# Out-projection of a trunk layer: low halves, S1 sums and one residual addition moved from GpSimd to VectorE

## The chip, the cores and the metric

One core of a Trainium2 chip runs the whole program. The metric is the device time of one execution in microseconds, lower is better. "VectorE" is DVE in the rows, "ScalarE" ACT, "GpSimd" POOL, "TensorE" PE; SP is the queue that issues the loads and stores.

## The reference

One layer, 1024 tokens of width 1024. A gated DeltaNet mixer (8 heads) and a cross-attention over 256 memory tokens (4 heads) give `y_mix` and `y_mem`; the part that matters here is what follows:

```
y = jnp.concatenate([y_mix, y_mem], axis=-1) @ w_out[layer]
h = h + rms_norm(y, norm_post_mix[layer])
f = swiglu(rms_norm(h, norm_pre_ffn[layer]), w_ffn_in[layer], w_ffn_out[layer])
h = h + rms_norm(f, norm_post_ffn[layer])
```

`y` is 1024 x 1536 times 1536 x 1024, all in float32.

## The kernel before

**Matmuls in three passes.** A float32 operand is split in two: ScalarE casts it to the short matmul type (the high half, `whi`), and another engine subtracts that from the float32 source (the low half, `wlo`). Each product is then three matmuls: high by high, high by low, low by high (`split_step`, lines 906 to 908). A matmul that reads a low half waits until its subtraction is done.

**The out-projection as seven block products.** `y` and `w_out` are cut into 2 x 2 blocks, and seven products of sums of blocks replace eight (`OPRODS`, `o_prod(j)` for j = 0 to 6). A block of the left operand (A11, A12, A21, A22) is 768 x 512, six k-blocks of 128 x 512; so is a block of the right one (B11, B12, B21, B22, and the weight sums T1 to T4, made early in the program and kept in DRAM). Product j takes six steps k. A step loads the A block and the B block (`o_operands`), has ScalarE cast both (line 890), makes both low halves (line 891), and then issues 4 x 3 matmuls into four accumulators. The high and low tiles have three buffers each, so the split can be at most about two steps ahead of TensorE.

In `o_operands` the two low halves go to different engines, the A block's to GpSimd and the B block's to VectorE:

```
for i, (src, eng) in enumerate(zip(srcs, (nc.gpsimd, nc.vector))):
    nc.scalar.copy(hi[:, i], src)
    last_lo[i] = eng.tensor_tensor(out=lo[:, i], in0=src, in1=hi[:, i].bitcast(F32), op=ALU.subtract).ins
```

**Sums of blocks.** `o_sums(1, k)` makes A11 - A21 on VectorE and S1 = A21 + A22 on GpSimd beside product 1; product 2 needs A22 - (A11 - A21) (`o_operands`, j = 2), product 3 uses S1 and makes a further difference of A12. All are additions of 128 x 512 tiles through the helper `add` (line 854). The blocks A21 and A22 lie in tiles named oB11h, oB11l and oB21h, two k-blocks of each in each tile.

**Results and residuals.** `o_combine` adds a finished accumulator (PSUM) to the partial results `hn` on VectorE, beside the first four steps of the next product, and ScalarE sums squares. In products 5 and 6 `post_stage` finishes the first half of the tokens, and behind product 6 the second half, one tile of 128 tokens at a time: three small GpSimd operations make `rstd` (lines 961, 83, 85), VectorE scales (line 965, 128 x 1024), then the residual `xr` is added (line 966, through `add`, 128 x 1024) and stored; ScalarE squares it (line 973), GpSimd makes the next `rstd`, ScalarE scales (line 981), and the tile's buffer can take the next load of `x`. `ON_POOL` lists the tiles, as (half, n), whose residual addition runs on GpSimd: one, (1, 0).

**What else runs there.** Beside product 0 the cross-attention still runs; beside products 1 to 3 the weights of the first FFN tile are prepared (`gate_w`, `up_w`: scaling at line 1057 and differences at line 1095 on VectorE, low halves at lines 93 and 1078 on GpSimd). Behind product 6 come the first FFN products `m1` and `m2`, whose second weight tile has its low half on VectorE (line 93), and the transposes of the normed tokens.

**Order.** Each engine takes its instructions in one order, fixed when the program is built: a scheduler places them from the order in the code and its own estimates, so moving an operation to another engine also moves its neighbours. An engine waits at the head of its queue.

In the rows the products start on TensorE at 688.84 us (0), 716.16 (1), 740.06 (2), 763.64 (3), 779.96 (4), 796.28 (5), 822.15 (6), and product 6 ends at 842.43.

Of the kernel before, what the change touches and what calls it, by code (L numbers as in the profile page):

```python
# [10 lines left out]
F32 = mybir.dt.float32  # L11
# [3 lines left out]
ALU = mybir.AluOpType  # L15
# [24 lines left out]

ON_POOL = ((1, 0),)
OB = 8
FILL = 2
TFILL = (3, 4)
# [8 lines left out]
def trunk_kernel(ctx: ExitStack, tc: tile.TileContext, a: dict, out: bass.AP):  # L55
    nc = tc.nc
# [122 lines left out]
    for tn in range(NT):  # L179
# [23 lines left out]
        for q in range(2):  # L203
            pt = bank(("ms", "iv")[q], "pt")
            for j in range(4):
# [3 lines left out]
            hi = uhi[hf][:, q * 4:q * 4 + 4, n * P:(n + 1) * P]  # L209
            nc.scalar.copy(hi, p3)  # L210
            nc.vector.tensor_tensor(out=ulo[hf][:, q * 4:q * 4 + 4, n * P:(n + 1) * P], in0=p3,
                                    in1=hi.bitcast(F32), op=ALU.subtract)
# [172 lines left out]
    def tmp(name):  # L385
# [38 lines left out]
                            in1=gc.rearrange("p h n -> p (h n)"), op=ALU.subtract)  # L424
# [428 lines left out]
    def add(out, x, y, eng=nc.vector, op=ALU.add):  # L853
        return eng.tensor_tensor(out=out, in0=x, in1=y, op=op)  # L854

    def load_block(t, name, k):
        if name[0] == "A":
            i, j = int(name[1]) - 1, int(name[2]) - 1
            src = y_d[k + KH * j][:, HO[i] * HF:(HO[i] + 1) * HF]
        else:  # L860
            src = t_d[name][k] if name[0] == "T" else wo_block(int(name[1]), int(name[2]), k)
        nc.sync.dma_start(t, src)

    def o_raw():
        return wp.tile([P, 2, HF], F32, tag="raw", name="raw", bufs=2)

    def block(name, k):
        if (name, k) not in oblk:
            t = yp.tile([P, HF], F32, name=f"{name}_{k}", bufs=1) if name in YP else free_slots.pop(0)
            oblk[name, k] = t  # L870
            load_block(t, name, k)
        return oblk[name, k]

    def o_operands(j, k):
        an, bn = OPRODS[j]
        first = j == 0 and k < 2
        raw = o_raw() if j == 6 or first else None
        if j == 2:

            add(block("A22", k), block("A22", k), block("A11", k), op=ALU.subtract)  # L880
        if raw is None:
            srcs = [block(an, k)]
        else:
            srcs = [raw[:, 0]]
            load_block(raw[:, 0], an, k)
        srcs.append(raw[:, 1] if first else yp.tile([P, HF], F32, tag="ob", name="ob", bufs=OB))
        load_block(srcs[1], bn, k)
        hi, lo = (wp.tile([P, 2, HF], F32R, tag="w" + c, name="w" + c, bufs=3) for c in ("hi", "lo"))
        for i, (src, eng) in enumerate(zip(srcs, (nc.gpsimd, nc.vector))):
            nc.scalar.copy(hi[:, i], src)  # L890
            last_lo[i] = eng.tensor_tensor(out=lo[:, i], in0=src, in1=hi[:, i].bitcast(F32), op=ALU.subtract).ins  # L891
        return hi, lo

    last_lo = [None, None]

    def o_sums(j, k):

        if j == 1:
            add(block("A11", k), block("A11", k), block("A21", k), op=ALU.subtract)
            add(block("A21", k), block("A21", k), block("A22", k), nc.gpsimd)  # L900
        elif j == 3:
            add(block("A12", k), block("A12", k), block("A22", k), op=ALU.subtract)

# [46 lines left out]
    def post_stage(i, half, n):  # L950
# [12 lines left out]
        elif i == 1:  # L963
            xr, rs = post[n]
            nc.vector.scalar_tensor_tensor(out=hn, in0=hn, scalar=rs, in1=grow[0], op0=ALU.mult, op1=ALU.mult)
            ins = add(xr, hn, xr, nc.gpsimd if (half, n) in ON_POOL else nc.vector).ins
            if (half, n) not in ON_POOL:
                last_h[0] = ins
# [38 lines left out]
    def o_prod(j):  # L1007
        acc = [bank((("pj", "sc"), ("ms", "iv"))[j % 2][n // 2], f"acc{j}") for n in range(4)]
        held = []
        for k in range(KH):  # L1010
            hl = o_operands(j, k)
            with tc.issue_after(last_lo[0]), tc.issue_after(last_lo[1]):
                o_sums(j, k)
                if j and k < 4:
                    o_combine(j - 1, k, oprev[0][k])
                if j >= 5:
                    t = k + KH * (j - 5)
                    for i in range(4):
                        post_stage(i, 0, t - POST[i])
            if j == 6 and k >= KH - TAIL:  # L1020
                held.append((k, hl))
                continue
            for n in range(4):
                mm = split_step(acc, n, k == 0, k == KH - 1, *hl)
                if j == 6 and k >= FILL:
                    with tc.issue_after(mm.ins):
                        next(fill, None)
# [440 lines left out]
```

## Time and profile before

| What | Value |
|---|---|
| Timed runs (3) | 1551.32, 1548.78, 1543.25 us; median 1548.78 |
| Profiled execution | 1535.88 us, span of its instructions 1533.7 us |
| Mean granted TensorE clock | 0.984 of full speed |
| Busy over the span | VectorE 1068.4 us (70%), ScalarE 682.1 (44%), GpSimd 825.6 (54%) |
| DMA | 168.13 MB, mean 110 GB/s |

The busy times are for the whole program; the out-projection, from 688.84 to 842.43 us, is a tenth of it. The profiled execution is one run of its own and lies 12.9 us below the median of the timed ones. A row's duration runs from an instruction's start to its end as recorded; where instructions follow each other without a gap, the distance of their starts is the better price.

### The profile page before, as it was taken

Reading aid. Unit: us, or ns where it says so; the run is one execution under the profiler, and the core shown is the slowest. Engines: PE = TensorE matmul, PEld = TensorE weight load, DVE = VectorE, ACT = ScalarE, POOL = GpSimd, SP = SyncE. Lnnn points to the kernel's source line nnn. Section 1 sums busy time; section 2 is a strip of 40 time slices with the busy share of each in tenths; the row PEclk is TensorE's granted clock in tenths of the full one; section 3 lists DMA queues with packets and bytes.
Section 4 is the critical chain, followed back from the end, with each engine's and each line's share of the span. In section 5 each row is a group of like instructions: output and inputs, shape, how many; then the busy total and the mean of one; then the engine's idle time right before and its main releaser. Section 6 shows DMA issues by size and latency. Waiting matters only on the chain.

```text
span 1533.7 us, 22655 instructions
## 1 busy us (share of the span) xinstructions
PE 1468.6 (96%) x8237; PEld 1207.5 (79%) x8237; DVE 1068.4 (70%) x1651; ACT 682.1 (44%) x1481; POOL 825.6 (54%) x705
## 2 busy tenths in 40 slices
PE   7999999999999999999798789999999999999996
PEld 5778888888888888887686668888888887778784
DVE  7555767677676867667977877666666665685967
ACT  7565555555555554345346532222222222444352
POOL 3543646474646544204756556666666665554455
PEclk9999999999999999999899899999999999999998
DMA  6411222222212220219334222222222223973334
GB/s 203 158 56 38 67 70 93 72 85 63 90 63 77 78 73 29 83 64 308 109 103 158 82 90 104 103 103 103 104 103 103 104 103 125 317 251 96 90 103 159
DMA packets 77553, 168.13 MB, mean 110 GB/s; under 512 B 10433, under 2 KB 12929, under 8 KB 77442
## 3 DMA queue, kind: packets, MB, share of 16 engines
q1 hardware_dynamic: 76720, 165.58, 32.1%
q8 instruction: 64, 1.05, 0.3%
q10 hardware_dynamic: 722, 1.12, 0.2%
q14 instruction: 47, 0.39, 0.1%
HBM read 124.42 MB, written 42.24 MB: 109 GB/s over the span
## 4 chain that ended last, share of the span: by engine, by line
PE 35%; DVE 5%; POOL 4%; issue 3%; DMA 2%; ACT 2%; DVEq 0%; SPq 0%; POOLq 0%; ACTq 0%
PE fo L907 3%; PE fo L908 3%; PE fo L906 3%; PE sc L137 3%; PE sc L135 2%; PE sc L136 2%; PE iv L135 2%; PE iv L137 2%; PE iv L136 2%; PE pj L136 2%; PE pj L137 2%; PE pj L135 2%; POOL wlo L891 2%; DVE B L854 1%; PE ms L136 1%
## 5 line engine op out<-in xcount | busy, mean ns | idle before, releaser
L246 PE MATMUL pj<-uhi,whi 128*128 128x512 f32 x496 | 216.3, 436 | 0.0
L93 POOL TENSOR_TENSOR wlo<-raw,whi 128x1024 fp32r<-128x1024 f32 x61 | 157.5, 2581 | 77.4 <-ACT whi L92 76.9
L246 PE MATMUL pj<-uhi,wlo 128*128 128x512 f32 x496 | 196.0, 395 | 0.0
L246 PE MATMUL pj<-ulo,whi 128*128 128x512 f32 x496 | 195.0, 393 | 0.0
L295 DVE SCALAR_TENSOR_TENSOR cv<-cb,convw_sb,cv 128x512 f32<-128x512 f32 x144 | 148.3, 1030 | 23.1 <-ACT cv L290 22.4
L1292 POOL TENSOR_TENSOR wlo<-ar,whi 128x512 fp32r<-128x512 f32 x75 | 106.4, 1421 | 98.0 <-ACT whi L1291 97.8
L907 PE MATMUL fo<-wlo,whi 128*128 128x512 f32 x308 | 123.3, 400 | 8.3 <-DVE wlo L1292 8.1
L908 PE MATMUL fo<-whi,wlo 128*128 128x512 f32 x308 | 120.8, 393 | 0.0
L906 PE MATMUL fo<-whi 128*128 128x512 f32 x308 | 118.4, 391 | 0.6 <-DVE c L854 0.6
L92 ACT CAST whi<-raw 128x1024 fp32r<-128x1024 f32 x66 | 69.6, 1054 | 106.1 <-DVE raw L1057 50.8
L1292 DVE TENSOR_TENSOR wlo<-B,whi 128x512 fp32r<-128x512 f32 x75 | 83.1, 1110 | 45.7 <-ACT whi L1291 45.1
L246 PEld LDWEIGHTS pj<-uhi,wlo 128*128 128x128 f32 x496 | 93.5, 189 | 21.5
L246 PEld LDWEIGHTS pj<-ulo,whi 128*128 128x128 f32 x496 | 94.4, 190 | 11.2
L246 PEld LDWEIGHTS pj<-uhi,whi 128*128 128x128 f32 x496 | 94.1, 190 | 11.3 <-issue 0.2
L1095 DVE TENSOR_TENSOR raw<-raw 128x512 f32<-128x512 f32 x86 | 84.8, 986 | 25.6 <-POOL wlo L93 17.1
L1057 DVE TENSOR_TENSOR raw<-raw,gcols_sb 128x1024 f32<-128x1024 f32 x44 | 67.2, 1527 | 50.0 <-DMA raw<-in_w_ffn_in 50.0
L1291 ACT CAST whi<-ar 128x512 fp32r<-128x512 f32 x75 | 46.5, 621 | 112.4 <-POOL wlo L1292 75.4
L907 PE MATMUL acc<-wlo,whi 128*128 128x512 f32 x168 | 69.1, 411 | 12.6 <-DVE wlo L891 12.6
L907 PEld LDWEIGHTS fo<-wlo,whi 128*128 128x128 f32 x308 | 58.1, 189 | 28.8 <-DVE wlo L1292 17.2
L1078 POOL TENSOR_TENSOR plo<-raw,phi 128x1024 fp32r<-128x1024 f32 (+1 forms) x22 | 52.7, 2397 | 46.2 <-ACT phi L1077 44.8
L908 PE MATMUL acc<-whi,wlo 128*128 128x512 f32 x168 | 68.7, 409 | 2.4 <-POOL wlo L891 2.4
L906 PEld LDWEIGHTS fo<-whi 128*128 128x128 f32 x308 | 58.2, 189 | 13.5 <-DVE c L854 1.0
(408 smaller groups left out, 4214.3 us busy)
## 6 DMA issues: line engine op xcount, KB each, us to landing
raw<-in_w_ffn_in SPq DMA_DIRECT2D x44, 512.0 KB, 3.3
raw<-in_w_in SPq DMA_DIRECT2D x36, 512.0 KB, 3.3
ar<-g_S SPq DMA_DIRECT2D x44, 256.0 KB, 2.6
B<-in_w_ffn_out SPq DMA_DIRECT2D x42, 256.0 KB, 4.7
g_A<-g SPq DMA_DIRECT2D x33, 256.0 KB, 2.0
ar<-g_A SPq DMA_DIRECT2D x29, 256.0 KB, 4.0
wsum<-in_w_out SPq DMA_DIRECT2D x24, 256.0 KB, 4.2
T_d<-wsum SPq DMA_DIRECT2D x24, 256.0 KB, 2.0
```

Source lines behind the costliest of these rows:

```text
L92: nc.scalar.copy(hi, raw)
L93: (lo_eng or nc.gpsimd).tensor_tensor(out=lo, in0=raw, in1=hi.bitcast(F32), op=ALU.subtract)
L135: nc.tensor.matmul(ps, whi, uhi, start=first, stop=False)
L136: nc.tensor.matmul(ps, whi, ulo, start=False, stop=False)
L137: return nc.tensor.matmul(ps, wlo, uhi, start=False, stop=last)
L246: ins = nc.tensor.matmul(*args, **kw)
L295: nc.vector.scalar_tensor_tensor(out=cf, in0=cb[:, c0:c0 + HF], scalar=w[:, j:j + 1], in1=cf, op0=ALU.mult, op1=ALU.add)
L906: nc.tensor.matmul(acc[n], hi[:, 0, ts_], hi[:, 1], start=first, stop=False)
L907: nc.tensor.matmul(acc[n], hi[:, 0, ts_], lo[:, 1], start=False, stop=False)
L908: return nc.tensor.matmul(acc[n], lo[:, 0, ts_], hi[:, 1], start=False, stop=last)
L1095: nc.vector.tensor_tensor(out=o, in0=x, in1=y, op=op)
L1292: last_lo[i] = eng.tensor_tensor(out=lo[:, i], in0=src, in1=hi[:, i].bitcast(F32), op=ALU.subtract).ins
```

## The change

All low halves of the out-projection, both operands' in all seven products, are made on VectorE (42 instructions that were GpSimd's), S1 as well (6), and no residual addition is left on GpSimd (1).

```
-ON_POOL = ((1, 0),)
+ON_POOL = ()
...
-        for i, (src, eng) in enumerate(zip(srcs, (nc.gpsimd, nc.vector))):
+        for i, src in enumerate(srcs):
             nc.scalar.copy(hi[:, i], src)
-            last_lo[i] = eng.tensor_tensor(out=lo[:, i], in0=src, in1=hi[:, i].bitcast(F32), op=ALU.subtract).ins
+            last_lo[i] = nc.vector.tensor_tensor(out=lo[:, i], in0=src, in1=hi[:, i].bitcast(F32), op=ALU.subtract).ins
...
         if j == 1:
             add(block("A11", k), block("A11", k), block("A21", k), op=ALU.subtract)
-            add(block("A21", k), block("A21", k), block("A22", k), nc.gpsimd)
+            add(block("A21", k), block("A21", k), block("A22", k))
```

VectorE in product 1, a piece of the difference (A_0 to A_2 are k-blocks of A11, A_3_8880 and A_4_8907 are of product 1's A12, `ob` is a B block, `oB11h` and `oB11l` hold A21 and A22):

```order
 L854 TENSOR_TENSOR A_0_8805<-A_0_8805,oB11h 128x512
-L891 TENSOR_TENSOR wlo<-ob,whi 128x512
+L854 TENSOR_TENSOR oB11h<-oB11h 128x512
+L891 TENSOR_TENSOR wlo<-A_3_8880,whi 128x512
 L854 TENSOR_TENSOR A_1_8834<-A_1_8834,oB11h 128x512
+L891 TENSOR_TENSOR wlo<-ob,whi 128x512
+L854 TENSOR_TENSOR oB11h<-oB11h 128x512
+L854 TENSOR_TENSOR A_2_8671<-A_2_8671,oB11l 128x512
+L891 TENSOR_TENSOR wlo<-A_4_8907,whi 128x512
+L854 TENSOR_TENSOR oB11l<-oB11l 128x512
```

Between two low halves of the B blocks there are now an S1 sum, a difference and the low half of an A block.

VectorE in product 5, before (acc_9257 is product 4's last accumulator, `hn` the partial results, `xr` a residual tile, `rstd` the row scale):

```order
L854 TENSOR_TENSOR hn<-acc_9257,hn 128x512
L965 SCALAR_TENSOR_TENSOR hn<-hn,rstd,grow_8786 128x1024
L891 TENSOR_TENSOR wlo<-ob,whi 128x512
L965 SCALAR_TENSOR_TENSOR hn<-hn,rstd,grow_8786 128x1024
L854 TENSOR_TENSOR xr<-hn,xr 128x1024
L891 TENSOR_TENSOR wlo<-ob,whi 128x512 x2
L854 TENSOR_TENSOR xr<-hn,xr 128x1024
```

and the same place now:

```order
L854 TENSOR_TENSOR hn<-acc_9257,hn 128x512
L965 SCALAR_TENSOR_TENSOR hn<-hn,rstd,grow_8786 128x1024
L891 TENSOR_TENSOR wlo<-A_4_8715,whi 128x512
L854 TENSOR_TENSOR xr<-hn,xr 128x1024
L891 TENSOR_TENSOR wlo<-ob,whi 128x512
L965 SCALAR_TENSOR_TENSOR hn<-hn,rstd,grow_8786 128x1024
L891 TENSOR_TENSOR wlo<-A_5_8737,whi 128x512
L891 TENSOR_TENSOR wlo<-ob,whi 128x512
L891 TENSOR_TENSOR wlo<-raw,whi 128x512
L854 TENSOR_TENSOR xr<-hn,xr 128x1024
```

The low halves of the A blocks stand between the residual operations, and the addition of the third tile has moved ahead of a low half and of the fourth tile's scaling.

VectorE behind product 6 (acc_9605 and acc_9606 are its last two accumulators, `c_9927` the first `m2` result, `wlo<-raw` the low half of the second FFN weight tile), before:

```order
L854 TENSOR_TENSOR hn<-acc_9605,hn 128x512
L854 TENSOR_TENSOR xr<-hn,xr 128x1024
L854 TENSOR_TENSOR hn<-acc_9606,hn 128x512
L965 SCALAR_TENSOR_TENSOR hn<-hn,rstd,grow_8786 128x1024
L93 TENSOR_TENSOR wlo<-raw,whi 128x1024
L965 SCALAR_TENSOR_TENSOR hn<-hn,rstd,grow_8786 128x1024
L1160 TENSOR_TENSOR c_9927<-pj,m_9912 128x512
L854 TENSOR_TENSOR xr<-hn,xr 128x1024 x2
```

and now:

```order
L854 TENSOR_TENSOR xr<-hn,xr 128x1024 x2
L854 TENSOR_TENSOR hn<-acc_9605,hn 128x512
L854 TENSOR_TENSOR hn<-acc_9606,hn 128x512
L1057 TENSOR_TENSOR raw<-raw,gcols_sb 128x1024
L965 SCALAR_TENSOR_TENSOR hn<-hn,rstd,grow_8786 128x1024
L1160 TENSOR_TENSOR c_9927<-pj,m_9912 128x512
L965 SCALAR_TENSOR_TENSOR hn<-hn,rstd,grow_8786 128x1024
L854 TENSOR_TENSOR xr<-hn,xr 128x1024
L93 TENSOR_TENSOR wlo<-raw,whi 128x1024
L854 TENSOR_TENSOR xr<-hn,xr 128x1024
```

The scaling of the second FFN weight tile (line 1057), which came earlier before, and its low half (line 93) now stand behind more of the residual work.

## Rows read from the trace of the kernel before

**Rows 1.** The page's first part: TensorE's busy time over the span.

```profile
PE 1468.6 (96%) x8237; PEld 1207.5 (79%) x8237; DVE 1068.4 (70%) x1651; ACT 682.1 (44%) x1481; POOL 825.6 (54%) x705
```

**Rows 2.** Busy time by stretch: products 0 to 6, then behind product 6.

```profile
core 0: us, PE busy (x) PEld busy (x) DVE busy (x) ACT busy (x) POOL busy (x), PEclk, DMA share, GB/s
688.84:716.16 27.32, 26.75 (x133) 20.73 (x131) 18.93 (x41) 15.99 (x43) 7.81 (x6) 1.00 0.83 278
716.16:740.06 23.90, 19.69 (x73) 14.90 (x72) 20.67 (x18) 8.49 (x15) 19.43 (x12) 0.86 0.65 223
740.06:763.64 23.58, 19.09 (x74) 14.41 (x72) 21.55 (x20) 11.41 (x23) 18.03 (x11) 0.93 0.38 123
763.64:779.96 16.32, 16.32 (x74) 13.52 (x72) 13.50 (x17) 6.84 (x12) 7.80 (x6) 1.00 0.32 96
779.96:796.28 16.32, 16.32 (x74) 13.52 (x72) 10.33 (x12) 7.57 (x14) 8.13 (x7) 1.00 0.32 97
796.28:822.15 25.87, 19.58 (x74) 14.90 (x72) 20.13 (x19) 15.83 (x29) 20.33 (x25) 0.88 0.47 164
822.15:842.43 20.28, 20.28 (x106) 16.84 (x104) 16.05 (x24) 14.90 (x31) 9.31 (x13) 0.99 0.42 142
842.43:864.73 22.30, 14.70 (x65) 11.21 (x63) 18.10 (x17) 13.17 (x23) 13.61 (x19) 0.90 0.38 142
```

**Rows 3.** TensorE's waits in products 1 and 2: us in total, times, longest.

```profile
PE acc L907 <- DVE wlo L891: 7.5, 4, 2.8
```

**Rows 4.** TensorE's waits in product 5.

```profile
PE acc L907 <- DVE wlo L891: 5.1, 2, 3.4
```

**Rows 5.** TensorE in order of time, product 1: start, duration, line [idle before].

```profile
731.14 0.79 PE L907 MATMUL acc<-wlo,whi 128*128 128x512 f32 x1 [2.84 <-DVE wlo L891]
731.73 0.63 PE L908 MATMUL acc<-whi,wlo 128*128 128x512 f32 x1
...
739.14 0.39 PE L908 MATMUL acc<-whi,wlo 128*128 128x512 f32 x1
```

**Rows 6.** VectorE in order of time, product 1.

```profile
722.54 1.78 DVE L854 TENSOR_TENSOR A<-A,oB11h 128x512 f32<-128x512 f32 x1
724.24 1.77 DVE L854 TENSOR_TENSOR oB11h<-oB11h,A 128x512 f32<-128x512 f32 x1
```

**Rows 7.** GpSimd in order of time, product 1.

```profile
723.73 1.73 POOL L891 TENSOR_TENSOR wlo<-A,whi 128x512 fp32r<-128x512 f32 x1
725.42 1.74 POOL L854 TENSOR_TENSOR oB11h<-oB11h 128x512 f32<-128x512 f32 x1
```

**Rows 8.** VectorE in order of time, product 6.

```profile
826.32 0.68 DVE L891 TENSOR_TENSOR wlo<-ob,whi 128x512 fp32r<-128x512 f32 x1
826.92 1.28 DVE L854 TENSOR_TENSOR hn<-acc,hn 128x512 f32<-128x512 f32 x2
```

**Rows 9.** GpSimd's groups in product 0: busy us, mean ns | idle before.

```profile
L891 POOL TENSOR_TENSOR wlo<-A,whi 128x512 fp32r<-128x512 f32 x6 | 7.8, 1302 | 36.5 <-DMA A<-y_d 19.9 <-ACT whi L890 11.3 <-DVE mx L775 5.4
```

**Rows 10.** VectorE in order of time, product 5.

```profile
803.57 1.23 DVE L854 TENSOR_TENSOR xr<-hn,xr 128x1024 f32<-128x1024 f32 x1
...
812.11 2.32 DVE L965 SCALAR_TENSOR_TENSOR hn<-hn,rstd,grow 128x1024 f32<-128x1024 f32 x1 [2.75 <-POOL rstd L85]
```

**Rows 11.** VectorE's groups in product 5.

```profile
L965 DVE SCALAR_TENSOR_TENSOR hn<-hn,rstd,grow 128x1024 f32<-128x1024 f32 x4 | 6.2, 1549 | 3.7 <-POOL rstd L85 3.6
```

**Rows 12.** GpSimd in order of time, product 2.

```profile
754.39 2.41 POOL L1078 TENSOR_TENSOR qlo<-raw,qhi 128x1024 fp32r<-128x1024 f32 x1
```

**Rows 13.** VectorE's waits from product 1 to product 6.

```profile
DVE A L854 <- DMA oB11h<-y_d: 1.9, 1, 1.9
```

**Rows 14.** VectorE in order of time, behind product 6.

```profile
841.97 3.42 DVE L965 SCALAR_TENSOR_TENSOR hn<-hn,rstd,grow 128x1024 f32<-128x1024 f32 x1 [0.40 <-POOL rstd L85]
```

**Rows 15.** TensorE in order of time, behind product 6.

```profile
850.60 0.50 PE L137 MATMUL ms<-B11h,wlo 128*128 128x512 f32 x1 [1.94 <-DVE wlo L93]
...
859.59 1.86 PE L991 MATMUL pt<-ident_sb,hn 128*128 128x128 f32 x10 [3.49 <-ACT hn L981]
```

## The prediction

> **What bounds the kernel now.** I read the page's busy shares first, then the busy time of every engine per product, then the waits of TensorE, and last the instructions in order of time in the places where TensorE waits. The busy share of TensorE [rows 1] says almost nothing here: it is a share over the whole program, and the change touches only the out-projection. Per product [rows 2] the reader is to see that products 3 and 4 take 16.32 us each, with TensorE busy for all of it. That is the price of one product when nothing is late (six steps of 2.72 us). Products 1, 2 and 5 have the same 72 matmuls, and take 23.90, 23.58 and 25.87 us. Product 6 has transposes between its matmuls and is full at 20.28 us. So products 1 to 6 take 126.27 us where 5 x 16.32 + 20.28 = 101.9 would do: **24.4 us are lost**, in products 1, 2 and 5. The waits name the culprit: low halves made on VectorE, in products 1 and 2 [rows 3] and in product 5 [rows 4]. The loss is larger than these waits, because the granted clock falls after each of the long ones (means 0.86, 0.93 and 0.88 [rows 2]): after the wait of 2.84 us a matmul takes 0.63 us where the others take 0.39, as at 1.2 instead of 2.4 GHz [rows 5].
>
> Why is VectorE late? In product 1 its additions start 1.70 us apart [rows 6], and so do GpSimd's beside them [rows 7]. In product 6, with GpSimd idle, the same VectorE form starts 0.60 us after the one before [rows 8] and the record says 0.68. An operation that reads two SBUF tiles on VectorE and one on GpSimd do not run side by side: together they take 1.70 us, about one after the other. GpSimd by itself takes 1.30 [rows 9]. The Trainium skill, SBUF — State Buffer, "Who interferes with whom", says the second of two such operations is blocked until the first ends; by that rule a pair would cost 1.30 + 0.60 = 1.90 us. The measured 1.70 decides, and by the rule each of the pairs below would save 0.2 us more.
>
> **The unit of the sum.** A pair costs 1.70 us now. Both operations on VectorE cost 2 x 0.60 = 1.20. Each moved operation that is paired with VectorE work therefore frees 0.50 us; one that ran while VectorE was idle costs VectorE 0.60. A wide operation (128x1024) alone is 1.23 [rows 10], I take 1.2.
>
> **Part by part.**
> - *Products 1 and 2* (47.48 us now, 32.64 needed by TensorE). VectorE has 18 + 20 operations there [rows 2]; the change adds 12 low halves and the 6 sums S1: 56, two of them wide scalings of line 1057. That is 54 x 0.60 + 2 x 1.2 = 34.8 us. GpSimd keeps the low half of line 93 and three of line 1078; one such ran 2.41 us [rows 12], and each can still hold VectorE for a pair's surplus of 1.1 us or, for the wide ones, about 1.8: at most 5.8, I take 3 since two of them fall into gaps or into product 3. 37.8, less one step (2.72) that three hi/lo buffers let VectorE run ahead, is 35.1; I take 35.5, a gain of **12.0**. Best: TensorE's 32.6, a gain of 14.8. Worst: VectorE also keeps the 5.3 us in which it now idles there (47.48 - 20.67 - 21.55), 43.1, a gain of 4.4. In the new order every S1 sum stands ahead of a low half in the queue, so a late block would hold the low halves behind it. The blocks' loads cost one wait of 1.9 us today [rows 13] and DMA is busy 0.65 of product 1, which is in the worst case.
> - *Products 3 and 4.* VectorE gets 17 + 12 + 12 = 41 operations, 24.6 us of 32.6: covered. GpSimd's line 1078 now meets the start of product 3, because that comes earlier; **-1.0** (0 to -4).
> - *Product 5.* 19 operations, eight of them wide (four residual tiles, each a scaling and an addition), and 6 low halves: 17 x 0.60 + 8 x 1.2 = 19.8. Less the lead of 2.72 it would be 17.1. But each tile's scaling needs its rstd from GpSimd; today one came 2.75 us late [rows 10], while GpSimd had low halves queued ahead of the small operations that make it. These low halves go. What remains is the chain square, three small operations, scaling. I leave 2.4 us for it: 19.5, a gain of **6.4**. Best 16.3, a gain of 9.5; worst all 3.7 us of rstd waits [rows 11] stay on top of the 19.8, a gain of 2.4.
> - *Product 6.* 24 + 6 operations, one wide, 18.6 us of 20.28: **0**.
> - *Behind product 6.* The addition of tile (1,0) moves: +1.2 us on VectorE. It ran beside a scaling that took 3.42 us [rows 14] where a wide operation alone takes 1.2, so 2.2 come back. But the low half of line 93 that TensorE awaits (1.94 us today [rows 15]) now stands behind two more additions, and TensorE's longest wait of the stretch, 3.49 us, is for a chain through the last residual tiles. I take **0** (+3 to -3).
> - *Product 0, beside the cross-attention.* Six low halves x 0.60 = 3.6 us more on VectorE, which is busy 18.93 of 27.32 us [rows 2], and its own low halves there get faster. These six waited 36.5 us in all on GpSimd, harmlessly [rows 9]; on VectorE a wait holds the attention's operations behind it. But ScalarE casts the A block right ahead of the B block, whose low half VectorE has always waited for, so the wait is not longer than today's. **-0.5** (+1 to -2).
>
> Sum: 12.0 - 1.0 + 6.4 + 0 + 0 - 0.5 = 16.9, say **17 us faster**. The profiled execution took 1535.88 us (span 1533.7), so it would take 1519; the three timed runs have a median of 1548.78, 12.9 above it, and since the terms are stalls of engines I take the same 17 off that: **1532**. All best ends together give 28, all worst ends -2; the forecast's own range is 5 to 26.
>
> **Rivals.**
> 1. *The waits change hands.* Products 1 and 2 stay tied to the arrival of the A21 and A22 blocks, and product 5 to its chain of square, rstd, scaling, addition, square, scaling and the load of the next tile. For it: one wait on DMA already [rows 13], rstd waits [rows 11]. Against it: after the first block VectorE never waits for a load in product 1. Then products 1 and 2 gain 4.4, product 5 2.4, products 3 and the rest lose 3: a gain of 4, **1545**, no change.
> 2. *VectorE is slow for reasons of its own*, and the stretched operations merely coincide with GpSimd's. Then 36 low halves at GpSimd's 1.30 and six sums at 1.70 come on top of the 102.2 us that VectorE is busy in products 1 to 6 [rows 2]: 102.2 + 46.8 + 10.2 = 159 against 126.3, **33 us slower, 1582**. It decides at 126.3 / 152 operations = 0.83 us for each: above that VectorE alone needs longer than the stretch takes now. Against it: product 6 shows 0.60 with ScalarE, TensorE and DMA all active [rows 2, 8]. The Trainium skill, Perfetto Trace Analysis, "Optimizing Scalar/DVE Operations", points this way: when VectorE is saturated, moving work to GpSimd may make sense. It adds that the two share a read port, so it might not help; the rows side with the addition [rows 6, 8].
>
> That the change doesn't do what it says is excluded by the order of the instructions: 42 low halves, six sums and one addition leave GpSimd.
>
> **The numbers.** A measurement of this kernel tells about 0.5%, 7.7 us, from no change. Forecast 0.79, nearly all of it over 7.7 us faster; rival 1 0.13, of which a little is faster; rival 2, and with it all that makes VectorE the bound, 0.08. That makes faster 0.79, same 0.13, slower 0.08. The range reaches from the forecast's better end (26 to 30 us, the runs themselves differing by 4 around their median) to rival 1: 1519 to 1546.
>
> **What would show it.** Right: low halves and sums of 0.68 us on VectorE in products 1 and 2, product 1 and 2 at 17 to 18.5 us each, product 5 at 18 to 21, granted clock near 1.00 there, GpSimd with no operation of line 891. Wrong: VectorE records above 0.83 us in products 1 and 2; TensorE waits of 2 us or more for a low half behind an S1 sum or a residual addition; product 0 longer than 28.5 us; a wait of over 5 us behind product 6.

## The result, and the profile after

The changed kernel took **1527.85 us** (median of 4 runs, 1522.9 to 1533.38) against 1546.01 for the kernel before beside it: a ratio of 0.9893, 95% interval 0.9857 to 0.9929. Its profiled execution took 1522.9 us with a span of 1521.1, where before it was 1535.88 and 1533.7.

The page's first part barely shows it [rows 1]: VectorE is as busy as before (1067.6 us, 1068.4 before) with 49 more instructions, GpSimd 71 us less.

```profile
PE 1462.8 (96%) x8237; PEld 1204.4 (79%) x8237; DVE 1067.6 (70%) x1700; ACT 682.9 (45%) x1481; POOL 754.2 (50%) x656
```

The busy time by stretch of the kernel after, products 0 to 6 and then the stretch up to the first product with B22; columns as in [rows 2]:

```profile
688.12:714.18 26.06, 26.06 (x134) 20.80 (x132) 20.07 (x47) 16.01 (x43) 0.00 (x0) 1.00 0.86 280
714.18:732.06 17.88, 17.25 (x74) 13.28 (x72) 15.83 (x24) 7.98 (x14) 2.40 (x1) 1.00 0.90 315
732.06:748.68 16.62, 16.62 (x73) 13.36 (x72) 16.62 (x28) 10.92 (x23) 1.24 (x1) 1.00 0.50 159
748.68:768.02 19.34, 16.92 (x74) 13.36 (x72) 18.79 (x26) 7.95 (x14) 6.14 (x3) 1.00 0.31 95
768.02:784.34 16.32, 16.32 (x74) 13.51 (x72) 10.17 (x18) 7.39 (x14) 0.00 (x0) 1.00 0.32 98
784.34:804.56 20.22, 16.91 (x74) 13.36 (x72) 16.81 (x21) 15.35 (x29) 10.96 (x18) 1.00 0.57 177
804.56:825.28 20.72, 20.34 (x105) 16.50 (x104) 19.08 (x31) 14.85 (x31) 3.09 (x7) 1.00 0.52 170
825.28:851.67 26.39, 17.76 (x70) 13.32 (x68) 18.99 (x19) 14.45 (x24) 13.38 (x19) 0.74 0.33 120
```

Products 1, 2 and 5 took 23.90, 23.58 and 25.87 us and now take 17.88, 16.62 and 20.22, each with a granted clock of 1.00. Product 3 takes 3.0 us more. Behind product 6 it went the other way: 842.43 to 865.07 (22.6 us) before, 26.39 now. In product 1 VectorE, in order of time, now reads

```profile
720.21 0.69 DVE L854 TENSOR_TENSOR oB11h<-oB11h 128x512 f32<-128x512 f32 x1
720.82 0.68 DVE L891 TENSOR_TENSOR wlo<-A,whi 128x512 fp32r<-128x512 f32 x1
721.42 0.69 DVE L854 TENSOR_TENSOR A<-A,oB11h 128x512 f32<-128x512 f32 x1
722.02 0.68 DVE L891 TENSOR_TENSOR wlo<-ob,whi 128x512 fp32r<-128x512 f32 x1
```

S1 sum, A low half, difference, B low half, all 0.60 us apart; in [rows 6] VectorE's additions stood 1.70 apart. The four operations are two former pairs: on VectorE alone they take 2.4 us, on the two engines side by side they took 3.4.

The 3.0 us of product 3 are in this piece of the kernel after, GpSimd and VectorE in order of time:

```profile
750.25 1.74 POOL L1078 TENSOR_TENSOR plo<-s,phi 128x512 fp32r<-128x512 f32 x1
...
750.76 1.79 DVE L891 TENSOR_TENSOR wlo<-ob,whi 128x512 fp32r<-128x512 f32 x1
...
751.96 2.87 POOL L1078 TENSOR_TENSOR qlo<-raw,qhi 128x1024 fp32r<-128x1024 f32 x1
...
752.47 2.91 DVE L854 TENSOR_TENSOR A<-A,oB11h 128x512 f32<-128x512 f32 x1
```

The low halves of line 1078, which nobody moved, now lie beside product 3's first steps and stretch VectorE from 0.69 to as much as 2.91 us. TensorE waits twice in product 3 for a low half, 2.4 us in all.

Behind product 6, TensorE's waits of the kernel after (us in total, times, longest) and the rows behind the second:

```profile
PE ms L135 <- ACT whi L92: 3.9, 1, 3.9
PE ms L137 <- DVE wlo L93: 3.8, 1, 3.8
```

```profile
837.39 1.22 DVE L854 TENSOR_TENSOR xr<-hn,xr 128x1024 f32<-128x1024 f32 x1
837.40 2.35 POOL L1078 TENSOR_TENSOR wlo<-raw,whi 128x512 fp32r<-128x512 f32 x1 [1.25 <-ACT whi L1077]
838.52 2.31 DVE L93 TENSOR_TENSOR wlo<-raw,whi 128x1024 fp32r<-128x1024 f32 x1
```

The low half that TensorE wants (line 93) stands behind a residual addition and is then stretched by GpSimd. Before, TensorE waited 1.94 us for it [rows 15]. The waits are not all of the 3.75 us, though. The same stretch before:

```profile
842.43:865.07 22.64, 15.04 (x67) 11.55 (x66) 18.44 (x17) 13.31 (x23) 13.95 (x19) 0.89 0.37 140
```

TensorE was without a matmul for 7.6 us then and for 8.6 now, 1.0 us more. The other 2.7 us are its matmuls, which took 15.04 us at a mean granted clock of 0.89 and take 17.76 at 0.74.

### The profile page after: what moved, and what is told of

The parts are those of the page before. It is cut to its first block, busy times and chain, and to the rows that moved or that the text cites. A ratio compares the mean times of both kernels' runs of the same rounds, so it can differ in the third digit from the quotient of the medians.

```text
span 1521.1 us, 22607 instructions
## 1 busy us (share of the span) xinstructions
PE 1462.8 (96%) x8237; PEld 1204.4 (79%) x8237; DVE 1067.6 (70%) x1700; ACT 682.9 (45%) x1481; POOL 754.2 (50%) x656
## 4 chain that ended last, share of the span: by engine, by line
PE 76%; DVE 10%; DMA 5%; issue 3%; POOL 3%; ACT 3%; SPq 1%; DVEq 0%; POOLq 0%; ACTq 0%
PE pj L246 21%; PE pj L135 3%; PE pj L137 3%; PE pj L136 3%; PE fo L907 3%; PE fo L908 3%; PE fo L906 3%; PE pc L246 3%; PE sc L137 3%; PE sc L135 3%; PE sc L136 2%; PE iv L135 2%; PE iv L137 2%; PE iv L136 2%; PE po L246 2%
## 5 line engine op out<-in xcount | busy, mean ns | idle before, releaser
L246 PE MATMUL pj<-ulo,whi 128*128 128x512 f32 x496 | 194.5, 392 | 0.0
L1077 ACT CAST phi<-raw 128x1024 fp32r<-128x1024 f32 (+1 forms) x22 | 22.8, 1034 | 100.9 <-PE sc L136 83.4
```

The costliest lines, as they stand in the source:

```text
L246: ins = nc.tensor.matmul(*args, **kw)
```

## The experiments

Four kernels at a time ran on one chip, with the kernel before beside them; ratios are to that kernel. "Block stretch" is the time from the first matmul of product 0 to the first with T4: 198.7 us before (688.84 to 887.57), 187.3 after.

**e1_lows_only** and **e2_sums_only** split the change: all 42 low halves on VectorE with sum and residual on GpSimd, and the reverse. The lines as they stand in the two kernels:

```
e1:  ON_POOL = ((1, 0),)
     add(block("A21", k), block("A21", k), block("A22", k), nc.gpsimd)
e2:  for i, (src, eng) in enumerate(zip(srcs, (nc.gpsimd, nc.vector))):
```

> Only the 42 low halves move to VectorE; the six S1 sums and the one residual addition stay on GpSimd. Shared-port theory (an operation with two SBUF inputs on VectorE and one on GpSimd take about 1.70 us together, one after the other): in product 1 VectorE has six operations less (3.6 us) but each sum holds it up for about 1.1 us (6.6), so product 1 grows from 17.9 to about 21 us, the rest is as in the full change: 3 us of the gain are lost, ratio to before 0.990 to 0.993. Dependency theory (the gain came from TensorE no longer waiting for GpSimd's slower low halves; a sum is awaited by nobody until product 3): the whole gain stays, ratio 0.989, product 1 at 17.9 us.

> The six S1 sums and the residual addition move to VectorE, the 42 low halves of the A blocks stay on GpSimd. Shared-port theory: six pairs of 1.70 us in product 1 become operations of 0.60 us more on VectorE, but the low halves still hold it up; product 1 falls from 23.9 to 19 to 22 us and the rest stays: 1 to 4 us faster, ratio 0.997 to 0.9995. Dependency theory: nothing that TensorE waits for has become faster, and VectorE has more to do: ratio 1.000 to 1.003.

Measured: e1 1527.27 us, ratio 0.9921 (0.9893 to 0.9949); e2 1533.95, 0.9948 (0.9920 to 0.9976). Their products 1 and 2, then 5, by stretch:

```profile
716.86:738.02 21.16, 17.23 (x74) 13.28 (x72) 20.03 (x19) 8.40 (x15) 12.24 (x7) 1.00 0.73 261
738.02:757.00 18.98, 17.34 (x73) 13.10 (x71) 17.34 (x25) 10.31 (x22) 4.36 (x3) 1.00 0.40 138
...
792.17:812.51 20.34, 16.96 (x73) 13.36 (x72) 16.87 (x22) 15.35 (x29) 10.98 (x18) 1.00 0.55 176
```

```profile
714.48:734.15 19.67, 16.62 (x73) 13.41 (x72) 19.02 (x22) 8.49 (x15) 13.13 (x6) 1.00 0.76 269
734.15:757.98 23.83, 17.55 (x74) 13.21 (x72) 23.24 (x23) 11.57 (x23) 18.84 (x11) 1.00 0.38 122
...
790.62:815.20 24.58, 19.01 (x74) 13.98 (x73) 19.12 (x19) 14.53 (x27) 20.06 (x24) 0.96 0.47 169
```

The low halves alone shorten the block stretch by 10.0 us (to 188.7), the sums alone by 4.2 (to 194.5), both by 11.4, which is 2.8 less than the parts together. It isn't lost where the pairs are: in products 1 and 2 the parts gave 7.3 and 4.0 us and both 13.0. It is lost at the end: from product 6's start to the first product with B22 it took 42.9 us before, 43.8 in e1, 43.7 in e2 and 47.1 with both. The sums, which only product 1 has, gave 4.2 us there and left product 2 at 23.83. Product 5 gained 5.5 us from the low halves alone and 1.3 in e2, where nothing that was moved runs in it. e1's product 1 of 21.16 us is what the shared port asks for, and not the 17.9 of the rival theory; e2 gained more than its forecast.

**e3_gp_read** and **e4_gp_write** test the cause. Both are the changed kernel with 42 further GpSimd operations, one per step, whose result nobody reads; they are meant to differ only in whether the operation reads SBUF. `still` is a constant tile. The added lines shift the numbers: line 854 is 856 here, 891 is 893.

```
+ nc.scalar.copy(beat[:, 0:1], hi[:, 1, 0:1].bitcast(F32))
+ nc.gpsimd.tensor_tensor(out=beat, in0=still, in1=still, op=ALU.add)    # e3
+ nc.gpsimd.memset(beat, 0.0)                                            # e4, in its place
```

> The full change, and GpSimd adds a constant SBUF tile to itself (128 x 512, two SBUF inputs) once in each of the 42 steps, into a tile that nobody reads; a one-column ScalarE copy starts it when the step's high halves are there. VectorE, ScalarE's casts and TensorE wait for none of it, and VectorE's order is that of the full change. Shared-port theory: VectorE records of 1.2 to 1.8 us come back in products 1, 2, 3 and 5; products 1 and 2 lose about 5 us each, product 3 about 3, product 5 about 4: ratio to before 0.998 to 1.003. Dependency theory: nothing waits for it, ratio 0.988 to 0.991.

> As the one before, but GpSimd only fills the tile (it reads no SBUF). Shared-port theory with the read side of the port as what is shared: VectorE records stay at 0.68 us, ratio to before 0.988 to 0.992, the same as the full change but for 42 small ScalarE copies and small GpSimd operations queued behind the fills. If any GpSimd activity slowed VectorE, reading or not, it would be 0.995 or more. Dependency theory: 0.988 to 0.991.

Measured: e3 1548.91 us, 1.0038 (1.0010 to 1.0066); e4 1528.45, 0.9906 (0.9870 to 0.9941). Product 1 in order of time, first e3, then e4:

```profile
725.13 0.68 DVE L856 TENSOR_TENSOR A<-A,oB11h 128x512 f32<-128x512 f32 x1
725.73 0.68 DVE L893 TENSOR_TENSOR wlo<-ob,whi 128x512 fp32r<-128x512 f32 x1
725.74 1.57 POOL L896 TENSOR_TENSOR beat<-still 128x512 f32<-128x512 f32 x1 [1.08 <-ACT beat L895]
726.33 1.52 DVE L856 TENSOR_TENSOR oB11h<-oB11h 128x512 f32<-128x512 f32 x1
```

```profile
722.87 0.69 DVE L893 TENSOR_TENSOR wlo<-A,whi 128x512 fp32r<-128x512 f32 x1
722.97 0.53 POOL L896 MEMSET beat<- 128x512 f32 x1 [2.19 <-ACT beat L895]
723.47 0.69 DVE L856 TENSOR_TENSOR oB11l<-oB11l 128x512 f32<-128x512 f32 x1
```

An addition on GpSimd that no one waits for stretches VectorE's next operation to 1.52 us; a write leaves it at 0.69. In products 0 to 6 of e3, 21 VectorE operations of this size took over 1 us with an added addition beside them; in e4 four did, and each of them stands beside a low half of line 93 or 1078. e3's block stretch is 203.0 us (689.02 to 892.05), longer than before the change; e4's is 187.5. So it is the reading of SBUF side by side, and no dependence between the engines' work, that the change removed. The two also differ in length (the write takes 0.53 us, the addition 1.0 to 1.8), and where GpSimd's small operations make `rstd`, a longer one queued ahead of them can cost too; products 1 to 3, which have none of those, lost 10.6 us in e3 and none in e4. The Trainium skill, SBUF — State Buffer, "Who interferes with whom", says that a VectorE operation with two SBUF inputs contends with a GpSimd operation that reads SBUF and not with one that only writes it; these two runs agree. Of the 20.5 us between the two medians 15.5 are the block stretch. The rest is not from here: e3's up projection, where nothing was added, lasted 418.6 us in its profile and e4's 408.5, and that is taken up below.

**full_again, e5_pin, e6_tail, e8_down** look for what was given back, and for the same pairs elsewhere. full_again is the changed kernel once more. e5 issues the low halves of line 1078 for the first FFN tile behind product 3's last cast; e6 prepares the second FFN weight tile ahead of the last residual work; e8 makes the change's edit in the FFN's down projection.

```
e5:  -if j == 5: up_w0(False)
     +if j == 4:
     +    with tc.issue_after(last_hi[0]): up_w0(False)
     ...                               # last_hi[0] is kept where line 890 casts
e6:  +raw1 = ffn_raw(KS[1], wp)            # j == 6, ahead of the last n loop
     +if n == 3: gate_w(1, raw1)           # in it, ahead of o_combine
e8:  -for i, (src, eng) in enumerate(((ar, nc.gpsimd), (b, nc.vector))):
     +for i, src in enumerate((ar, b)):    # and nc.vector below
```

> The changed kernel itself once more, beside the next three on one chip, so that they can be set against it. Expected: a ratio of 0.986 to 0.992 to the kernel before, and the same lengths of the products as in its first profile to within 0.3 us: 26.1, 17.9, 16.6, 19.3, 16.3, 20.2 and 20.7 us.

> The changed kernel, with the first FFN weights' preparation (the three GpSimd lows of L1078) issued behind product 3's last ScalarE rounding, one product later. Theory: product 3's 3.0 us more come from these three lows holding VectorE's additions and subtractions. Then product 3 falls from 19.3 to 16.3 to 17.0 us, product 4, where VectorE has fewer operations, stays at 16.3 to 17.0, and the whole is 2 to 3 us below the changed kernel (0.998 to 0.9985 of it). Rival, that product 3 is late for its own six differences and the block loads: product 3 stays over 18.5 us wherever the lows stand, and the whole stays within 1 us.

> The changed kernel, with the second gate weight's load, scaling and rounding issued ahead of the last token tile's residual work behind product 6, not behind it. Theory: the 3.75 us that were given back behind product 6 are the two waits of TensorE for that weight (3.9 us for its high half on ScalarE, 3.85 us for its low half on VectorE), which stand behind VectorE's additions. Then both fall under 1.5 us, the stretch from product 6's end to the first product with B22 falls from 26.4 to 21 to 24 us, and the whole is 2 to 5 us below the changed kernel. Rival, that the chain of norms and residuals sets that stretch anyway: the waits move to the transposes behind it, the stretch stays at 25.5 us or more, and the whole within 1 us.

> The changed kernel, with the same edit made in the FFN's down projection too: its 75 low halves of the first operand go from GpSimd to VectorE. Theory, that two engines reading SBUF hold each other wherever they subtract side by side: the 75 GpSimd subtractions of 1.4 us go, VectorE's of that line fall from a mean of 1.09 us to 0.7 to 0.8, TensorE's waits for these lows (some 23 us by the groups of waits) fall by 5 to 15 us, and the whole is 5 to 8 us below the changed kernel. Rival, that the waits there are for the loads or for ScalarE's roundings: the waits take another releaser's name, and the whole stays within 1.5 us. Rival, that VectorE has no room there: over 2 us slower.

Measured: full_again 1530.47 us, ratio 0.9924 (0.9893 to 0.9955); e5 1530.95, 0.9910 (0.9876 to 0.9943); e6 1533.80, 0.9952 (0.9926 to 0.9979); e8 1524.68, 0.9892 (0.9850 to 0.9934). The stages say more than the medians here.

*full_again* repeated products 0 to 4 and 6 to within 0.3 us, but product 5 took 22.10 us in it, not 20.22. That was missed. TensorE waited 0.3 us more there, and its matmuls took 18.50 us at a mean granted clock of 0.92, 16.91 at 1.00 in the first profile.

*e5* brought product 3 to what TensorE needs, and product 4 lost 0.3 us:

```profile
750.58:766.90 16.32, 16.32 (x74) 13.52 (x72) 16.13 (x22) 8.74 (x15) 5.80 (x3) 1.00 0.30 96
766.90:783.50 16.60, 16.60 (x74) 13.36 (x73) 12.86 (x21) 7.40 (x14) 1.24 (x1) 1.00 0.38 112
```

The three low halves did not leave product 3: GpSimd has 5.80 us of them in it. They run from 761.10 on, at its end, and there they still stretch VectorE's low halves to 2.65, 1.79 and 1.78 us. TensorE waits for none of these: VectorE, undisturbed until then, had got ahead of it.

*e6*: the waits for the second weight tile (7.7 us in the kernel after) went, and others of 10.1 us stood behind them. From product 6's start to the first product with B22 it is 47.40 us, 46.68 in full_again: for this stretch the rival held. The block stretch was 185.3 us, 4.1 below full_again's, in product 5 and behind B22; e12, below, shows that this doesn't come with the edit. TensorE's waits there:

```profile
PE pt L991 <- ACT hn L981: 5.8, 2, 5.0
PE pt L991 <- DVE t L1181: 4.3, 2, 3.0
```

*e8*: the down projection took 217.6 us (from its first matmul to its last) and 225.7 in full_again, 8.1 less. The instructions of its line, full_again and then e8 (duration in ns: min/median/max):

```profile
L1292 POOL TENSOR_TENSOR wlo<-ar,whi x75: 1292/1302/1864, 1293.7 to 1504.4; 128x512 fp32r<-128x512 f32 x75
L1292 DVE TENSOR_TENSOR wlo<-B,whi x75: 676/1321/1795, 1294.2 to 1507.3; 128x512 fp32r<-128x512 f32 x75
```

```profile
L1292 DVE TENSOR_TENSOR wlo<-ar,whi x75: 676/691/694, 1302.2 to 1509.8; 128x512 fp32r<-128x512 f32 x75
L1292 DVE TENSOR_TENSOR wlo<-B,whi x75: 676/685/693, 1302.8 to 1510.4; 128x512 fp32r<-128x512 f32 x75
```

TensorE's wait for them fell from 8.7 us (12 times) to 3.5 (5 times). e8's median is 5.8 us below full_again's, inside its forecast of 5 to 8; those of e5 and e6 are 0.5 and 3.3 above it, where 2 to 3 and 2 to 5 below were forecast. In the profiles of all three the FFN's **up projection**, which none of them touches, lasted longer: 418.4, 416.4 and 419.2 us, and 408.9 in full_again. One round of it, full_again and then e5, VectorE and GpSimd in order of time:

```profile
1033.52 0.68 DVE L1095 TENSOR_TENSOR raw<-raw 128x512 f32<-128x512 f32 x1
...
1034.29 2.41 POOL L1078 TENSOR_TENSOR plo<-raw,phi 128x1024 fp32r<-128x1024 f32 x1 [1.42 <-ACT phi L1077]
```

```profile
1032.47 2.93 POOL L1078 TENSOR_TENSOR plo<-raw,phi 128x1024 fp32r<-128x1024 f32 x1
1033.06 2.89 DVE L1095 TENSOR_TENSOR raw<-raw 128x512 f32<-128x512 f32 x1
```

Where GpSimd's low half starts after VectorE's last addition, both run freely. Where it starts a little earlier, the addition takes 2.89 us, the sums behind it are late, and TensorE then waits for `qlo`. In e5 that happens in 8 of the 20 rounds, mostly every second one, and TensorE waits 8 times, 11.3 us; in full_again it never happens, and TensorE waits once, 3.5 us. It is the same pair as in the out-projection.

**e9_resid, e10_plo, e11_all, e12_all_tail.** e9 puts the residual addition of tile (1,0) back on GpSimd. e10 moves `plo` of the up projection to VectorE (20 operations). e11 is e5, e8 and e10 together, e12 adds e6.

```
e9:  ON_POOL = ((1, 0),)
e10: -halves(("S1", "S2"), p, 0, u, 8)
     +halves(("S1", "S2"), p, 0, u, 8, nc.vector if k > 1 else nc.gpsimd)
     ...                               # halves passes the engine on
```

> The changed kernel with one operation put back: the residual of the last half's first token tile (L965's partner, 128x1024) on GpSimd, as before. Theory: with it on VectorE the additions behind product 6 stand in one line, and from product 6's start to the first product with B22 it took 47.1 us, with it on GpSimd and the lows moved 43.8 us. Then that stretch is 43.3 to 44.5 us here too, and the whole 2 to 4 us below the changed kernel. Rival, that the 43.8 us came with the sums on GpSimd: the stretch stays at 46.5 to 47.5 us, and the whole within 1 us.

> The changed kernel with 20 of the FFN up projection's subtractions of L1078 (plo, 128x1024) on VectorE too. In the profiles so far the up projection lasts either 408 to 409 us or 416 to 419 us. Theory: in the longer form GpSimd's plo starts before VectorE's last addition of L1095 and stretches it from 0.68 to 2.9 us, in every second turn or so, and the high half of q and its low half are late by 1.1 to 2.6 us each time. With plo on VectorE the two can't meet: the up projection lasts 407 to 410 us, TensorE waits for qlo once and not eight times, the runs lie closer together (all within 8 us), and the median is 2 to 6 us below the changed kernel. Rival, that VectorE has no room for 20 more subtractions of 1.2 us: TensorE waits for plo or for a sum, and the up projection lasts 412 us or more. Rival, that the long form has another cause: both forms stay.

> The changed kernel with three further edits: the first FFN weights' lows one product later, the down projection's first operand's lows on VectorE, and plo of the up projection on VectorE. If the parts add: 2.6 us (product 3, 19.3 to 16.3), 8.1 us (down projection 225.7 to 217.6) and 0 to 8 us (the long form of the up projection) below the changed kernel: 1511 to 1521 us, a ratio of 0.980 to 0.986 to the kernel before. Rival, that what is gained in one stage is lost in the next: 1522 us or more, over 0.987.

> The kernel with those three edits, and also the second gate weight's preparation ahead of the last residual work behind product 6. In its own run that took 2 to 4 us out of the stretch from product 0 to the first product with T4 (185.3 us beside 187.3 and 189.4). If it holds without the long form of the up projection: 1509 to 1519 us, 1 to 3 us below the kernel with the three edits alone. Rival, that the chain of norms sets that stretch: within 1 us of it.

| Kernel | Median, us | Ratio (95%) | Block stretch | Up projection | Down projection |
|---|---|---|---|---|---|
| full_again | 1530.47 | 0.9924 (0.9893 to 0.9955) | 189.4 | 408.9 | 225.7 |
| e9_resid | 1529.50 | 0.9910 (0.9880 to 0.9941) | 184.7 | 419.8 | 226.8 |
| e10_plo | 1525.07 | 0.9899 (0.9869 to 0.9928) | 187.2 | 408.2 | 226.5 |
| e11_all | 1516.79 | 0.9845 (0.9811 to 0.9878) | 185.6 | 407.9 | 216.8 |
| e12_all_tail | 1515.20 | 0.9836 (0.9803 to 0.9870) | 185.6 | 407.8 | 216.3 |

full_again stands here from the group before, on another chip (the kernel before: 1543.77 us there, 1542.65 here).

*e9*: from product 6's start to the first product with B22 44.22 us, as forecast, 47.11 in the changed kernel: 2.9 us of what was given back (2.5 beside full_again) hang on this one addition. In e2 the same addition is on VectorE too and the stretch takes 43.7, so it costs this only together with the moved low halves, in the order that the two make. VectorE in e9:

```profile
835.79 1.28 DVE L965 SCALAR_TENSOR_TENSOR hn<-hn,rstd,grow 128x1024 f32<-128x1024 f32 x1 [1.51 <-POOL rstd L85]
837.00 1.22 DVE L93 TENSOR_TENSOR wlo<-raw,whi 128x1024 fp32r<-128x1024 f32 x1
838.13 2.32 DVE L854 TENSOR_TENSOR xr<-hn,xr 128x1024 f32<-128x1024 f32 x1
```

The low half of line 93 stands ahead of the residual addition again, takes 1.22 us, and TensorE's second wait is gone (the first is 5.9 us). The median shows nothing of it, under the long form of the up projection in its profile.

*e10*: its up projection had the short form, TensorE waited 2.9 us for `qlo`, in three times, not one as forecast, and its six runs lie within 4.7 us (1522.55 to 1527.28; full_again's twelve within 16.5, the five each of e11 and e12 within 7.2). e10, e11 and e12 all show 407.8 to 408.2 us, the five profiles that went over 416 are of kernels without this edit. Since six other profiles were short as well, three short ones make it likely, not certain, that the long form is out.

*e11* adds up as forecast and is the best of what can be told apart: 1.55% under the kernel before. *e12* is within 1.6 us of it with the same block stretch, so the second weight tile's place brings nothing that these runs can show. A kernel with e9's and e11's edits together wasn't run.

## Why the prediction was right

- **The unit.** A pair of 1.70 us becoming two of 0.60 is shown, on both sides: by the rows of the kernel after (0.60), and by e3, where reading GpSimd operations bring VectorE's 1.5 us back. One reading under it was wrong: in product 6 GpSimd was not idle beside the row that gave the 0.60 [rows 8]. It made two low halves there,

```profile
825.08 3.08 POOL L891 TENSOR_TENSOR wlo<-raw,whi 128x512 fp32r<-128x512 f32 x2 [2.29 <-ACT whi L890]
```

  and VectorE's low half at 826.32 took 0.68 us all the same; GpSimd's two took 0.48 us more than two by themselves [rows 9]. The price of 0.60 holds by the kernel after, where GpSimd is idle; the row showed that a pair doesn't always cost VectorE anything.
- **Products 1 and 2:** 12.0 forecast, 13.0 measured (47.48 to 34.50), 1.9 above what TensorE needs. TensorE waits there for a low half once, 0.6 us; 7.5 before [rows 3]. The one wait for a block, 1.36 us, is the first difference's, as before, and no S1 sum waited for one. The forecast held 3 us here for the low halves of lines 93 and 1078; most of line 1078 has moved into product 3, so this term and the next belong together: 11.0 forecast, 10.0 measured.
- **Products 3 and 4:** -1.0 forecast, -3.0 measured, inside 0 to -4. The mechanism was named, line 1078 against product 3, and undersized: all three of its low halves reach into product 3 (6.14 us of GpSimd in its stretch), at its start, and with them at its end the 3.0 us are gone (e5).
- **Product 5:** 6.4 forecast, 5.65 measured, and 3.8 in full_again. It stays the least certain term: in the kernel after, a low half stood behind a residual addition that had waited 1.89 us, and TensorE waited 2.62 us for that low half. That is one of the prediction's signs of being wrong, and it fits rival 1's chain. What the addition waited for isn't shown; its tile's load of `x` was issued at 793.40, 4.6 us ahead of it, and the next one took 4.1 us to land.
- **Product 6:** 0 forecast, 0.4 us lost.
- **Behind product 6:** 0 forecast (+3 to -3), -3.75 measured, just outside. The step that failed is the sum that came to 0. The 2.2 us did come back, the scaling runs in 1.28 us now; but the delay of line 93, named beside them, was priced, with the chain's, at the 1.0 us that is left of them after the moved addition's 1.2. TensorE waits 3.8 us for line 93 and 3.9 for the high half ahead of it, the same sign of being wrong, and its clock was lower (0.74, 0.89 before). With the addition alone put back, 2.9 us return (e9); the rest stays open. A further 1.3 us, in no term of the sum, went up to T4 (22.5 to 23.8).
- **Product 0:** -0.5 forecast, 1.3 gained; it came with the low halves (26.00 us in e1, 27.29 in e2).

By the two profiles the block stretch gained 11.4 us where the terms said 16.9, and the span 12.6. The runs say 18.2 (1546.01 to 1527.85), full_again's 13.3 (1543.77 to 1530.47). The forecast of 17 lies between them, but its closeness to 18.2 isn't all merit: the terms of the out-projection came to 5.5 us less than forecast, and the runs carry a stage outside of it that lasts one of two lengths 10 us apart. Which length each timed run had can't be seen, so what it adds to the 18.2 stays open. But the 18.2 rest on four runs of the kernel before that all lie at 1542.8 to 1551.3 us, while of the 75 runs of it beside the experiments 35 lie at 1534 to 1539.3 and 40 at 1541 to 1551. The two profiles both have the short up projection (409.2 and 408.3 us), and they are 13.0 us apart, as the medians beside full_again are. The gain is rather 13 us than 18, the sum was some 4 us too high, and that the forecast and the first measurement agree within 1.2 us is luck.

**The rivals.** Waits did change hands, but behind product 6 (3.75 us with the clock) and in product 5 (2.62 us), not in products 1 and 2. That VectorE is slow for reasons of its own is out: with both engines' low halves and sums in products 1 and 2 it starts one every 0.60 us, once the blocks are there. The Trainium skill, Perfetto Trace Analysis, "Optimizing Scalar/DVE Operations", warns that offloading between these two engines might not help because of the shared read port; here taking the work back gained, and the trace agrees with the warning.

## What to carry to other kernels

When VectorE has operations with two SBUF inputs and GpSimd reads SBUF beside them, price them together, as a pair (1.70 us here), and ask what both would cost on VectorE alone (1.20): VectorE can be the fuller engine and still be the better place. Look in every stage for the same pair before going further in one; the down projection held 8.1 us of it. Such low halves cost most at the start of a product, where VectorE has no lead (3.0 us in product 3), and little at its end (0.3 us in e5). After such a move, see what GpSimd work slides beside the freed stretch, and whether the moved operation now stands ahead of something that TensorE awaits.

## What the runs showed of the hardware

- VectorE is not always the one that is held. In e2 a GpSimd low half took 6.53 us, for as long as VectorE's additions and low halves followed each other without a gap:

```profile
729.56 0.68 DVE L854 TENSOR_TENSOR oB11l<-oB11l 128x512 f32<-128x512 f32 x1
729.65 6.53 POOL L891 TENSOR_TENSOR wlo<-oB11h,whi 128x512 fp32r<-128x512 f32 x1 [4.78 <-ACT whi L890]
730.16 0.68 DVE L854 TENSOR_TENSOR A<-A,oB21h 128x512 f32<-128x512 f32 x1
```

  It ended at 736.18, 1.2 us after VectorE had turned to an accumulator in PSUM (734.98). What decides between taking turns at 1.70 us and holding one engine off was not tested.
- The smallest GpSimd operations are held too: in the kernel after, a 128x1 addition took 0.19 us at 822.46 and 1.23 at 823.71, beside VectorE's 128x1024 scaling.
- A stage of equal rounds can run in one of two orders of the same pair: the up projection took 408 to 409 us, or 416 to 420, in e5 with VectorE's addition stretched to 2.89 us in 8 of its 20 rounds.
